# A decoder trunk in float32: the pools of SBUF tiles are placed in another order

## The chip, the cores and the metric

The kernel runs on 1 core of one Trainium2 chip. The metric is the device time of one execution in microseconds (us). Before the change it is 1981.16 us, the median of 3 runs (1981.11 to 1984.77).

## The reference, cut to what matters

Two layers work on `x` of 512 positions by 1024 channels. Everything is float32.

```python
for l in range(2):
    x = x + 0.5 * swiglu(rmsnorm(x, ln_ffn1[l]), w_ffn1_gu[l], w_ffn1_down[l])   # 1024 -> 2 x 2816 -> 1024
    h = rmsnorm(x, ln_mix[l])
    u_pool, q, k, v, gate_logits = split(h @ w_in[l])          # 512, 512, 128, 128, 2048 columns
    a = pool_mixer(u_pool, pool_w[l], pool_scale[l]) @ w_pool_branch[l]
    b = sliding_window_attention(rope(rmsnorm(q)), rope(rmsnorm(k)), v, sinks[l]) @ w_attn_branch[l]
    g_pool, g_attn = split(sigmoid(gate_logits))
    x = x + (g_pool * a + g_attn * b) @ w_out[l]
    x = x + 0.5 * swiglu(rmsnorm(x, ln_ffn2[l]), w_ffn2_gu[l], w_ffn2_down[l])
```

## The kernel before

`x` stays in SBUF as 8 tiles of 128 channels by 512 positions. Every large product is made of three matmuls: both operands are split into a high part (type float32r, a rounded float32) and a low part (what is left), and high times high, low times high and high times low are added up in PSUM (`term`, or the innermost loop of `product`). Names that end in `h` are high parts, in `l` low parts: `wh`, `wl` the weights, `xgh`, `xgl` the normed input, `hh`, `hl` the input of the down product, `ah`, `al` the attention's output, `yh`, `yl` the input of the output projection. `dh`, `dl` are the pool mixer's small products.

A matmul has a stationary operand, which is loaded into the array, and a moving operand, which streams past it column by column. In the rows of the trace a matmul reads `out<-moving,stationary`. Which one moves differs by stage:

- up product of an FFN (`product`, called by `block`): the weights move (512 or 384 columns), `xgh` and `xgl` are stationary. It uses seven products of half size in place of eight, and so some weight tiles are sums of others (`sums`). The qkv product is made the same way round with 256 columns.
- down product (`down`): `hh` and `hl` move (512 columns), the weights are stationary.
- `u` and gate products (`tile_of`): `xgh` and `xgl` move, the weights are stationary.
- branch products (the loop over `br` in `mix`): for each of 8 output tiles first four terms in which `ph` and `pl` move, then four in which `ah` and `al` move. `ph` and `pl` are the pool mixer's result; they lie behind the first 16 KB of the tiles `xgh` and `xgl` (`nm.spare`), and the trace shows them under those names.
- output product: `yh` and `yl` move.
- transposes (`turned`, `heads`, `attend`): the identity, a part of `cst`, moves, and what is transposed is stationary.

Weights come by DMA into a ring of six tiles `raw` (pool `rw`, SP's queue; the sums of two weight blocks by an adding DMA of POOL's queue). ScalarE casts them into `wh` (4 tiles in turn), VectorE subtracts into `wl` (3 tiles in turn). `Weights.prep` does this after each product for tiles some places ahead. At the end of each stage `Norm.split` makes the next stage's `xgh` and `xgl` out of each finished tile of `x`; `Norm.square` adds up the squares. Each stage has its pools: `ffn` opens `hp` (`hh`, `hl`), `ep`, `er` and `sums`, `mix` opens `mp` and `rp`, and they close with the stage. Engines work in the order in which the code is written, since every instruction is recorded with `keep_in_program_order` (line 90, which is the line in all rows).

A pool lies behind the pools that were opened before it. The built program places the tiles as in the table under "The change".

Of the kernel before, what the change touches and what calls it, by code (L numbers as in the profile page):

```python
# [9 lines left out]
F32 = mybir.dt.float32  # L10
F32R = mybir.dt.float32r
# [7 lines left out]
P = 128  # L19
L = 2  # L20
S = 512
# [3 lines left out]
HT = S // 2  # L25
# [5 lines left out]
NB = S // P  # L31
HQ = 8
HKV = 2
G = 4
HD = 64
# [5 lines left out]
TB = 6  # L41
RING = 16
RAW = 6
HI, LO = 4, 3
# [57 lines left out]
def trunk(ctx, tc, xT, consts, vecs, rows, w_g4, w_g3, w_d8, w_d6, w_qkv, w_u, w_pool, w_gate, w_br, w_out, out):  # L102
    nc = Engines(tc)
    pool = lambda name, bufs, **kw: ctx.enter_context(tc.tile_pool(name=name, bufs=bufs, **kw))
    cp, rw, wh_, wl_, xp = pool("cp", 1), pool("rw", RAW), pool("wh", HI), pool("wl", LO), pool("xp", 1)
    tp, sp = pool("tp", TB), pool("sp", 2)
    pa = pool("pa", 1, space=PSUM)

    cst = cp.tile([P, C_N], F32, name="cst")
# [21 lines left out]
    def temp(name, dt=F32):  # L131
        return tp.tile([P, S], dt, name=name, tag="t")

    def split(hi, lo, src, scale=None):

        if scale is None:
            nc.scalar.copy(out=hi, in_=src)
            nc.vector.tensor_tensor(out=lo, in0=src, in1=hi.bitcast(F32), op=ALU.subtract)
        else:
            nc.scalar.activation(out=hi, in_=src, func=AF.Copy, scale=scale)  # L140
            nc.vector.scalar_tensor_tensor(
                out=lo, in0=src, scalar=scale, in1=hi.bitcast(F32), op0=ALU.mult, op1=ALU.subtract
            )
# [165 lines left out]
    class Norm:  # L309
# [5 lines left out]
        def split(self, k):  # L315
            g = self.gain[:, k:k + 1]
            if self.h is None:
                self.h = xp.tile([P, 7 * 4 * HT], F32R, name="xgh")
                self.l = xp.tile([P, 7 * 4 * HT], F32R, name="xgl")
                self.spare = [t[:, KT * S:] for t in (self.h, self.l)]  # L320
                if self.halves:
                    self.h, self.l = (t.rearrange("p (i k t) -> p i k t", i=7, k=4) for t in (self.h, self.l))
                else:
                    self.h, self.l = (t[:, :KT * S].rearrange("p (k t) -> p k t", k=KT) for t in (self.h, self.l))
            if not self.halves:
                split(self.h[:, k, :], self.l[:, k, :], x[:, k, :], scale=g)
                return
            j = k % 4
            of = lambda i, n=1: (t[:, i:i + n, j, :] for t in (self.h, self.l))
            two = lambda t: t.rearrange("p (i t) -> p i t", t=HT)  # L330
            if k < 4:
                split(*of(B11), two(x[:, k, :])[:, 0:1, :], scale=g)
                d = temp("d")[:, :HT]
                nc.vector.tensor_tensor(out=d, in0=x[:, k, :HT], in1=x[:, k, HT:], op=ALU.subtract)
                split(*of(T1), two(d), scale=g)
                return
            xg, t, u = temp("xg"), temp("t23"), temp("t4")[:, :HT]
            gj = self.gain[:, j:j + 1]
            nc.scalar.activation(out=xg, in_=x[:, k, :], func=AF.Copy, scale=g)
            bh, bl = of(B21, 2)  # L340
            nc.scalar.copy(out=bh, in_=two(xg))
            nc.vector.scalar_tensor_tensor(
                out=t[:, HT:], in0=x[:, j, HT:], scalar=gj, in1=xg[:, HT:], op0=ALU.mult, op1=ALU.subtract
            )
            nc.vector.scalar_tensor_tensor(
                out=t[:, :HT], in0=x[:, j, :HT], scalar=gj, in1=t[:, HT:], op0=ALU.mult, op1=ALU.subtract
            )
            nc.vector.tensor_tensor(out=u, in0=xg[:, :HT], in1=t[:, :HT], op=ALU.subtract)
            nc.vector.tensor_tensor(out=bl, in0=two(xg), in1=bh.bitcast(F32), op=ALU.subtract)
            split(*of(T2, 2), two(t))  # L350
            split(*of(T4), two(u))
# [44 lines left out]
    def ffn(ctx, nm, nxt, last):  # L396
# [93 lines left out]
        def turned(src, b, base, n, hid, q):  # L490

            pt = pa.tile([P, S], F32, name=("pt_tp", "pt_pv")[q])
            for j in range(n // P):
                nc.tensor.transpose(pt[:, j * P:(j + 1) * P], src[:, j * P:(j + 1) * P], ident)
            split(
                *(t[:, base:base + n // P, b * P:(b + 1) * P] for t in hid),
                pt[:, :n].rearrange("p (j t) -> p j t", t=P),
            )
# [51 lines left out]

    @with_exitstack
    def mix(ctx, l, nm, nxt):
        mp = ctx.enter_context(tc.tile_pool(name="mp", bufs=1))
        rp = ctx.enter_context(tc.tile_pool(name="rp", bufs=RING))
        bank["mm"] = ctx.enter_context(tc.tile_pool(name="ps", bufs=4, space=PSUM))
        psc = ctx.enter_context(tc.tile_pool(name="psc", bufs=1, space=PSUM))
        gains = row[:, l, 0:HD], row[:, l, HD:2 * HD]
# [2 lines left out]

        wph, wpl = (t[:, 4 * S:5 * S] for t in nm.spare)
        us = [rp.tile([P, S], F32, name="u", tag="r") for _ in WIN]
        kv = mp.tile([P, NB, 4, HD], F32, name="kv")
        qT = mp.tile([P, G, S], F32, name="qT")
        kT = mp.tile([P, S], F32, name="kT")
        ph, pl = (t[:, :4 * S].rearrange("p (k t) -> p k t", k=4) for t in nm.spare)
        ah, al = (mp.tile([P, 4, S], F32R, name=n) for n in ("ah", "al"))
        nsink = sp.tile([P, HQ], F32, name="nsink")
        nc.vector.tensor_scalar(out=nsink, in0=sinks, scalar1=-1.0, scalar2=None, op0=ALU.mult)

# [3 lines left out]
        def window(g):  # L574

            w, cur, step = WIN[g], us[g], 1
            while step < w:
                nx = temp("win")
                nc.vector.tensor_copy(out=nx[:, :step], in_=cur[:, :step])
                nc.vector.tensor_tensor(out=nx[:, step:], in0=cur[:, step:], in1=cur[:, :S - step], op=ALU.add)  # L580
                cur, step = nx, step * 2
            yield
            nc.vector.tensor_tensor(
                out=cur[:, 0:16], in0=cur[:, 0:16], in1=cst[:, C_WC + g * 16:C_WC + (g + 1) * 16], op=ALU.mult
            )
            d = temp("d")
            nc.vector.scalar_tensor_tensor(
                out=d, in0=cur, scalar=1.0 / w, in1=us[g], op0=ALU.mult, op1=ALU.subtract
            )
            dh, dl = temp("dh", F32R), temp("dl", F32R)  # L590
            split(dh, dl, d)
            yield
            pt = mm()
            gemm(pt, [(wph[:, g * P:(g + 1) * P], wpl[:, g * P:(g + 1) * P], dh, dl)])
            yield
            split(ph[:, g, :], pl[:, g, :], pt, scale=vec[:, l, 3 * KT + g:3 * KT + g + 1])
            yield

        def rotate(z, n, cos, sin):
# [4 lines left out]
            nc.vector.tensor_tensor(out=rb[..., 0:8], in0=z[..., 8:16], in1=sin[..., 0:8], op=ALU.mult)  # L604
            nc.vector.tensor_tensor(out=rb[..., 8:16], in0=z[..., 0:8], in1=sin[..., 8:16], op=ALU.mult)
            nc.vector.tensor_tensor(out=z[..., 0:ROT], in0=ra, in1=rb, op=ALU.add)

        rs = mp.tile([P, NB, HQ], F32, name="hrs")

        ssq = mp.tile([P, NB, HQ], F32, name="hss")  # L610

        def sums(z, out):

# [242 lines left out]
    for l in range(L):  # L856
        nxt = Norm(gain(l, 1), False)
        ffn(nm, nxt, False)
        nm, nxt = nxt, Norm(gain(l, 2), True)
        mix(l, nm, nxt)  # L860
        nm, nxt = nxt, (Norm(gain(l + 1, 0), True) if l + 1 < L else None)
        ffn(nm, nxt, l + 1 == L)
        nm = nxt
# [72 lines left out]
```

## Time and profile before

| | |
|---|---|
| median of 3 runs | 1981.16 us |
| the profiled execution | 1982.2 us |
| its span (first to last instruction) | 1980.2 us |
| TensorE matmuls busy | 1920.4 us, 97% of the span |
| VectorE busy | 1304.4 us, 66% |
| ScalarE busy | 852.2 us, 43% |
| GpSimd busy | 132.9 us, 7% |
| mean granted clock of TensorE | 0.988 of full speed |
| HBM traffic | 130 GB/s |

How to read it: the profiled execution took 1.0 us more than the median, and 2.0 us of it lie outside the span. The duration of a single matmul in the rows contains its way through the array and overlaps with the next one's; what a matmul costs in a row of matmuls is the distance from its start to the next one's start. The chain that ended last gives that best: a piece of it is so many matmuls that follow one another without a wait, with the time that they took together.

### The profile page before, as it was taken

What the parts mean: (1) busy time and instruction counts of PE and PEld (TensorE: products, weight loads), DVE (VectorE), ACT (ScalarE), POOL (GpSimd) and SP (SyncE); (2) the same over time, 40 slices, a digit from 0 to 9 for tenths busy, and PEclk for the clock granted to TensorE, in tenths of its full rate; (3) what the DMA queues carried; (4) which work ended last, traced back from release to release, by engine and by line L of the source; (5) the groups of instructions that cost most, each with busy time, mean ns of one, the idle gap of its engine ahead of it and who ended that gap; (6) DMA issues with size and microseconds to landing.
All of it is one profiled execution on the core that took longest, in us unless ns stands there. A gap on an engine that the chain in (4) does not pass through costs nothing.

```text
span 1980.2 us, 24215 instructions
## 1 busy us (share of the span) xinstructions
PE 1920.4 (97%) x9240; PEld 1611.0 (81%) x9240; DVE 1304.4 (66%) x1884; ACT 852.2 (43%) x1286; POOL 132.9 (7%) x134
## 2 busy tenths in 40 slices
PE   3999999999999999999989999999999999999999
PEld 2788889897778788889868888898977877888897
DVE  5765747667756774756787476576765677657474
ACT  5433525445534542433454244244454454335242
POOL 3000000000001100000020000000000021000000
PEclk6999999999999999999999999999999999999999
DMA  5655546422224554646546564553222237455452
GB/s 173 178 148 150 160 107 160 128 92 75 75 86 117 149 160 128 181 120 148 134 119 179 140 172 124 127 154 119 90 64 86 85 87 204 139 151 165 117 157 78
DMA packets 77348, 258.48 MB, mean 131 GB/s; under 512 B 8720, under 2 KB 8720, under 8 KB 77232
## 3 DMA queue, kind: packets, MB, share of 16 engines
q1 hardware_dynamic: 63072, 210.27, 32.6%
q0 software_dynamic: 13872, 46.28, 13.9%
q8 instruction: 72, 1.18, 0.3%
q14 instruction: 44, 0.36, 0.1%
q10 hardware_dynamic: 288, 0.39, 0.1%
HBM read 254.81 MB, written 2.10 MB: 130 GB/s over the span
## 4 chain that ended last, share of the span: by engine, by line
PE 92%; DVE 5%; ACT 2%; issue 0%; DMA 0%; POOL 0%; SPq 0%; ACTq 0%; POOLq 0%
PE mm L90 86%; PE sc L90 3%; PE pt_pv L90 2%; PE pt_tp L90 2%; DVE wl L90 2%; DVE xgl L90 1%; ACT xgh L90 1%; DVE x L90 1%; DVE t L90 1%; DMA raw<-in_w_g 0%; DVE ssq L90 0%; ACT wh L90 0%; POOL ssq L90 0%; DVE v L90 0%; ACT xg L90 0%
## 5 line engine op out<-in xcount | busy, mean ns | idle before, releaser
L90 ACT CAST wh<-raw 128x1024 fp32r<-128x1024 f32 (+1 forms) x420 | 417.9, 995 | 567.6 <-PE mm L90 536.3
L90 DVE TENSOR_TENSOR wl<-raw,wh 128x1024 fp32r<-128x1024 f32 (+1 forms) x420 | 495.2, 1179 | 158.7 <-PE mm L90 83.3
L90 PE MATMUL mm<-wh,xgh 128*128 128x512 f32 (+2 forms) x1440 | 532.4, 370 | 25.4 <-DVE x L90 9.0
L90 PE MATMUL mm<-wl,xgh 128*128 128x512 f32 (+2 forms) x1440 | 529.1, 367 | 1.2 <-DVE wl L90 1.2
L90 PE MATMUL mm<-wh,xgl 128*128 128x512 f32 (+2 forms) x1440 | 528.7, 367 | 0.0
L90 PEld LDWEIGHTS mm<-wh,xgh 128*128 128x128 f32 x1440 | 272.7, 189 | 64.4 <-ACT wh L90 21.7
L90 PEld LDWEIGHTS mm<-wl,xgh 128*128 128x128 f32 x1440 | 272.8, 189 | 37.3 <-DVE wl L90 2.0
L90 PEld LDWEIGHTS mm<-wh,xgl 128*128 128x128 f32 x1440 | 272.6, 189 | 35.8
L90 PE MATMUL mm<-hh,wl 128*128 128x512 f32 x704 | 279.9, 398 | 2.6 <-DVE wl L90 2.6
L90 PE MATMUL mm<-hh,wh 128*128 128x512 f32 x704 | 281.6, 400 | 0.0
L90 PE MATMUL mm<-hl,wh 128*128 128x512 f32 x704 | 279.5, 397 | 0.0
L90 DVE SCALAR_TENSOR_TENSOR x<-mm,x 128x512 f32<-128x512 f32 x96 | 66.3, 690 | 215.3 <-PE mm L90 215.3
L90 POOL DMA_DIRECT2D raw<-in_w_g x96 | 82.1, 858 | 1700.9 <-DMA raw<-in_w_g 757.2
L90 ACT CAST wh<-sums 128x1024 fp32r<-128x1024 f32 (+1 forms) x96 | 94.1, 980 | 197.6 <-PE mm L90 140.7
L90 PEld LDWEIGHTS mm<-hh,wl 128*128 128x128 f32 x704 | 133.0, 189 | 35.8 <-DVE wl L90 3.5
L90 PEld LDWEIGHTS mm<-hh,wh 128*128 128x128 f32 x704 | 133.0, 189 | 31.2
L90 PEld LDWEIGHTS mm<-hl,wh 128*128 128x128 f32 x704 | 132.9, 189 | 31.3
L90 PE MATMUL mm<-xgh,wh 128*128 128x512 f32 x384 | 154.8, 403 | 1.8 <-DVE x L90 1.8
L90 PE MATMUL mm<-xgh,wl 128*128 128x512 f32 x384 | 150.1, 391 | 0.0
L90 PE MATMUL mm<-xgl,wh 128*128 128x512 f32 x384 | 149.9, 390 | 0.0
L90 DVE TENSOR_TENSOR wl<-sums,wh 128x1024 fp32r<-128x1024 f32 (+1 forms) x96 | 106.7, 1131 | 12.8 <-PE mm L90 12.6
L90 PEld LDWEIGHTS mm<-xgh,wh 128*128 128x128 f32 x384 | 72.1, 188 | 22.5 <-issue 8.2
(174 smaller groups left out, 1979.6 us busy)
## 6 DMA issues: line engine op xcount, KB each, us to landing
raw<-in_w_g SPq DMA_DIRECT2D x160, 512.0 KB, 3.9
raw<-in_w_g POOLq DMA_DIRECT2D x64, 512.0 KB, 6.2
raw<-in_w_d SPq DMA_DIRECT2D x64, 512.0 KB, 3.4
raw<-in_w_g SPq DMA_DIRECT2D x80, 384.0 KB, 3.2
raw<-in_w_gate SPq DMA_DIRECT2D x32, 512.0 KB, 3.5
raw<-in_w_g POOLq DMA_DIRECT2D x32, 384.0 KB, 5.1
raw<-in_w_d SPq DMA_DIRECT2D x32, 384.0 KB, 3.1
raw<-in_w_br SPq DMA_DIRECT2D x16, 512.0 KB, 3.5
```

Of the source, the lines that this page charges most:

```text
L90: return lambda *args, **kw: self.tc.keep_in_program_order(call(*args, **kw))
```

## The change

No instruction is added, removed or moved, and no wait: both built programs hold the same instructions in the same order on each engine, with the same semaphores and values. What differs is where tiles lie in a partition. The pools `wh`, `wl` and a new pool `xl` for `xgh` and `xgl` are opened first and on the left side, the other pools of the trunk on the right side, which fills the partition from its end. In `mix` the tiles `ah` and `al` get a pool of their own ahead of `rp` (`u`, `z`, `q`, `yh`, `yl`), and `rp` goes ahead of `mp`.

```diff
-    cp, rw, wh_, wl_, xp = pool("cp", 1), pool("rw", RAW), pool("wh", HI), pool("wl", LO), pool("xp", 1)
-    tp, sp = pool("tp", TB), pool("sp", 2)
+
+    wh_, wl_, xl = pool("wh", HI, side="left"), pool("wl", LO, side="left"), pool("xl", 1, side="left")
+    cp, rw, xp = pool("cp", 1, side="right"), pool("rw", RAW, side="right"), pool("xp", 1, side="right")
+    tp, sp = pool("tp", TB, side="right"), pool("sp", 2, side="right")
...
-                self.h = xp.tile([P, 7 * 4 * HT], F32R, name="xgh")
-                self.l = xp.tile([P, 7 * 4 * HT], F32R, name="xgl")
+                self.h = xl.tile([P, 7 * 4 * HT], F32R, name="xgh")
+                self.l = xl.tile([P, 7 * 4 * HT], F32R, name="xgl")
...
+        ap = ctx.enter_context(tc.tile_pool(name="ap", bufs=1))
+        ah, al = (ap.tile([P, 4, S], F32R, name=n) for n in ("ah", "al"))
+        rp = ctx.enter_context(tc.tile_pool(name="rp", bufs=RING))
         mp = ctx.enter_context(tc.tile_pool(name="mp", bufs=1))
-        rp = ctx.enter_context(tc.tile_pool(name="rp", bufs=RING))
```

The rest of the diff opens `rs`, `ssq` and `kv` in another order inside `mp`. Where the tiles lie, in KB (1024 bytes) from the start of a partition, by the built programs:

| tiles | moving operand in | before | after |
|---|---|---|---|
| `wh` (4), `wl` (3) | FFN up, qkv | 37.66 to 65.66 | 8.12 to 36.12 |
| `xgh` / `xgl` | `u`, gate, branch (`ph`, `pl`) | 81.66 to 109.66 / to 137.66 | 36.12 to 64.12 / to 92.12 |
| `hh` / `hl` | down | 160.81 / 176.81, each 16 long | 92.12 / 108.12 |
| `ah` / `al` | branch | 174.81 / 182.81, each 8 long | 92.12 / 100.12 |
| `yh`, `yl` (8 each, 2 long) | output | 191.06 to 223.06 | 108.12 to 140.12 |
| `dh`, `dl`, `p`, `diag` and other temporaries | small products | 141.69 to 153.69 | 162.41 to 174.41 |
| `cst` (identity, masks) | transposes | 8.12 to 10.88 | 218.44 to 221.19 |
| `v`, `r` (FFN), stationary in transposes | - | 200.81 to 212.81 | 132.12 to 144.12 |
| `x` | - | 65.66 to 81.66 | 174.41 to 190.41 |
| `raw` (6) | - | 13.66 to 37.66 | 194.44 to 218.44 |
| `sums` (2) | - | 212.81 to 220.81 | 144.12 to 152.12 |

The trunk's tiles before start 32 bytes past a multiple of 64 bytes up to and including `xgl`, and on a multiple of 64 from the temporaries on. After the change those of the first five rows start on a multiple of 64.

## Rows read from the trace of the kernel before

**Rows 1.** The page: busy time, share and instructions of each engine, and the chain that ended last by engine.

```profile
PE 1920.4 (97%) x9240; PEld 1611.0 (81%) x9240; DVE 1304.4 (66%) x1884; ACT 852.2 (43%) x1286; POOL 132.9 (7%) x134
PE 92%; DVE 5%; ACT 2%; issue 0%; DMA 0%; POOL 0%; SPq 0%; ACTq 0%; POOLq 0%
```

**Rows 2.** Groups of matmuls by form over the whole span: out<-moving,stationary, size, count, busy us, mean ns of one. Each product of a stage stands in three groups (high by high, low by high, high by low) of one count; one or two of them are shown.

```profile
L90 PE MATMUL mm<-wh,xgh 128*128 128x512 f32 x896 | 354.8, 396 | 25.4 <-DVE x L90 9.0 <-DVE v L90 5.9 <-ACT wh L90 5.8
L90 PE MATMUL mm<-hh,wh 128*128 128x512 f32 x704 | 281.6, 400 | 0.0
L90 PE MATMUL mm<-hl,wh 128*128 128x512 f32 x704 | 279.5, 397 | 0.0
L90 PE MATMUL mm<-xgh,wh 128*128 128x512 f32 x384 | 154.8, 403 | 1.8 <-DVE x L90 1.8
L90 PE MATMUL mm<-wh,xgh 128*128 128x384 f32 x448 | 150.4, 336 | 0.0
L90 PE MATMUL mm<-yh,wh 128*128 128x512 f32 x128 | 50.8, 396 | 0.0
L90 PE MATMUL mm<-wh,xgh 128*128 128x256 f32 x96 | 27.2, 283 | 0.0
L90 PE MATMUL mm<-ah,wh 128*128 128x512 f32 x64 | 25.2, 394 | 0.0
```

**Rows 3.** Pieces of the chain that ended last: start us, us, what, count of matmuls. The pieces are of an up product with 512 columns, of transposes, of an up product with 384 columns, of a qkv product with 256 columns, of the gate's last tile with the branch and the output products, and of the last down product.

```profile
90.55 32.67 PE mm L90 x144
123.22 0.44 PE pt_tp L90 x4
...
329.30 24.99 PE mm L90 x144
...
414.28 2.88 PE mm L90 x24
...
558.88 92.29 PE mm L90 x396
...
1946.97 29.53 PE mm L90 x126
```

**Rows 4.** TensorE in order of time in one tile of the branch product: start us, us. Nine matmuls with `ph` or `pl` moving (shown as `xgh`, `xgl`) lie between the first row and the first `ah` row, twelve with `ah` or `al` between that and the last row. The two `xgl` rows have their moving operand at 129.66 and 131.66 KB.

```profile
573.47 0.39 PE L90 MATMUL mm<-xgh,wh 128*128 128x512 f32 x1
...
574.37 0.39 PE L90 MATMUL mm<-xgl,wh 128*128 128x512 f32 x1
...
575.05 0.39 PE L90 MATMUL mm<-xgl,wh 128*128 128x512 f32 x1
...
575.50 0.40 PE L90 MATMUL mm<-ah,wh 128*128 128x512 f32 x1
...
578.31 0.39 PE L90 MATMUL mm<-xgh,wh 128*128 128x512 f32 x1
```

**Rows 5.** The same view in the gate product: three matmuls of the gate, three of the pool mixer (`dh`, `dl`, between 141.69 and 153.69 KB), and the next of the gate.

```profile
439.23 0.39 PE L90 MATMUL mm<-xgh,wh 128*128 128x512 f32 x1
...
439.90 0.40 PE L90 MATMUL mm<-dh,xgh 128*128 128x512 f32 x1
...
440.61 0.39 PE L90 MATMUL mm<-xgh,wh 128*128 128x512 f32 x1
```

**Rows 6.** Groups of VectorE's subtraction and of ScalarE's cast by form. `raw` lies at 13.66 to 37.66 KB, `sums` at 212.81 to 220.81 KB.

```profile
L90 DVE TENSOR_TENSOR wl<-raw,wh 128x1024 fp32r<-128x1024 f32 x308 | 385.3, 1251 | 119.3 <-PE mm L90 56.8 <-issue 27.9 <-ACT sa L90 15.6
L90 DVE TENSOR_TENSOR wl<-sums,wh 128x1024 fp32r<-128x1024 f32 x64 | 76.8, 1220 | 10.8 <-PE mm L90 10.6
...
L90 ACT CAST wh<-raw 128x1024 fp32r<-128x1024 f32 x308 | 324.1, 1052 | 445.8 <-PE mm L90 416.2 <-PE sc L90 11.9 <-issue 7.0
L90 ACT CAST wh<-sums 128x1024 fp32r<-128x1024 f32 x64 | 67.3, 1052 | 129.1 <-PE mm L90 82.3 <-DVE sums L90 46.8
```

**Rows 7.** DMA issues: what, queue, count, size of one, median us from issue to landing. `praw` lies among the temporaries.

```profile
raw<-in_w_g SPq DMA_DIRECT2D x160, 512.0 KB, 3.9
...
praw<-in_w_pool SPq DMA_DIRECT2D x2, 256.0 KB, 3.8
```

**Rows 8.** The chain that ended last at the end of the first FFN (to 390.20) and at the end of layer 0's second FFN: start us, us, what.

```profile
364.05 0.70 DVE x L90
...
389.40 0.66 DVE x L90
390.06 0.14 issue
390.20 1.86 PE mm L90 x7
...
976.18 0.70 DVE x L90
...
1012.49 0.61 DVE x L90
1013.24 3.71 PE mm L90 x8
```

**Rows 9.** Stretches: from:to us, length, busy time of PE, PEld, DVE, ACT and POOL, PEclk (granted clock as a share of full speed), DMA share, GB/s.

```profile
965.00:1023.00 58.00, 48.05 (x201) 38.25 (x200) 44.09 (x68) 29.21 (x50) 13.36 (x9) 0.91 0.34 95
...
1630.00:1645.00 15.00, 12.75 (x53) 10.37 (x52) 10.96 (x20) 8.40 (x10) 1.96 (x3) 0.89 0.69 162
```

More of the change, by code (lines that the diff above doesn't have):

```diff
@@ L562, in mix @@
         us = [rp.tile([P, S], F32, name="u", tag="r") for _ in WIN]
-        kv = mp.tile([P, NB, 4, HD], F32, name="kv")
+        rs = mp.tile([P, NB, HQ], F32, name="hrs")
+        ssq = mp.tile([P, NB, HQ], F32, name="hss")
         qT = mp.tile([P, G, S], F32, name="qT")
@@ L566, in mix @@
         ph, pl = (t[:, :4 * S].rearrange("p (k t) -> p k t", k=4) for t in nm.spare)
-        ah, al = (mp.tile([P, 4, S], F32R, name=n) for n in ("ah", "al"))
+        kv = mp.tile([P, NB, 4, HD], F32, name="kv")
         nsink = sp.tile([P, HQ], F32, name="nsink")
@@ L606, in rotate @@
             nc.vector.tensor_tensor(out=z[..., 0:ROT], in0=ra, in1=rb, op=ALU.add)
-        rs = mp.tile([P, NB, HQ], F32, name="hrs")
-        ssq = mp.tile([P, NB, HQ], F32, name="hss")
         def sums(z, out):
```

## The prediction, made before the changed kernel was run

> **What bounds the kernel now.** I read the page first: its busy times and its chain by engine. TensorE's matmuls fill 97% of the span and make 92% of the chain that ended last; VectorE is at 66%, ScalarE at 43% [rows 1]. So the price of a matmul in a row of matmuls is what the kernel pays, and the forms tell how many there are of each [rows 2]. Their mean durations (396, 400, 403 ns) overlap and say little. The pieces of the chain give the spacing [rows 3]. An up product with 512 columns (the weights move, from 37 to 66 KB) takes 32.67 us for 144 matmuls, 226.9 ns each. The last down product (`hh` and `hl` move, from 160 to 193 KB) takes 29.53 us for 126 with as many columns, 234.4 ns each. Neither piece holds a wait, so the 7.5 ns are TensorE's own.
>
> Is it the place, or the kind of product? The branch product answers: weights stationary, 512 columns, one PSUM tile after another, and only the moving operand changes in the middle. Nine matmuls with `ph` and `pl` take 575.50 - 573.47 = 2.03 us, 226 ns each; the twelve with `ah` and `al` (175 to 191 KB) that follow take 578.31 - 575.50 = 2.81 us, 234 ns each [rows 4]. The pool mixer's `dh` and `dl` (142 to 154 KB) show the same: three take 0.71 us, 237 ns each, after three of the gate's in 0.67 us [rows 5]. Moving operands that begin at 141 KB or more are slow, those from 37 to 134 KB are fast. The two `pl` rows at 129.66 and 131.66 KB lie above 128 KB, each between two low ones, and the nine show no delay [rows 4]: the edge is not sharply at 128 KB, or one such matmul alone is hidden.
>
> **The change part by part.**
>
> *Matmuls whose moving operand comes down.* Down: 3 x 704 = 2112. Output: 3 x 128 = 384. Branch, attention's half: 3 x 64 = 192 [rows 2]. 2688 in all, at 234.4 - 226.9 = 7.5 ns: -20.2 us. A check on the largest mixed piece: 12 gate and 96 `ph`/`pl` matmuls at 226.9 ns and 96 + 192 others at 234.4 ns make 92.0 us, the piece has 92.29 [rows 3].
>
> *The tail of `yh` and `yl`.* Six of the sixteen tiles lie above 128 KB afterwards, two of them above 136 KB. Each of the eight pairs has 48 of the 384 matmuls. If the edge is at 128 KB, three pairs stay slow: 144 x 7.5 = 1.1 us. By the `pl` rows only the pair at 136 and 138 KB is in doubt: 48 x 7.5 = 0.4 us. I take +0.4, with 0 and 1.1 as its ends.
>
> *Matmuls whose moving operand goes up.* `cst` goes from 8 to 218 KB; the transposes use it, 128 columns each, some 450 of them, 0.44 / 4 = 110 ns each [rows 3]. If the extra time goes with the columns, 7.5 x 128 / 512 = 1.9 ns, that is +0.9 us at most. Against it, what they load as the stationary operand (`v`, `r`) comes down by 60 KB; no row shows what that is worth, and 1.9 ns each is its bound too. I take 0, between -0.9 and +0.9. Matmuls with `kT`, `p`, `dh`, `dl` or `diag` stay above 140 KB: 0.
>
> *The stationary operands.* `wh`, `wl`, `xgh`, `xgl` go down; `xgl` as a stationary operand already lies on both sides of 128 KB in the up products that run at 226.9 ns: 0.
>
> *VectorE and ScalarE.* `raw`, `x` and `cst` go up. The subtraction takes 1251 ns from `raw` (low) and 1220 from `sums` (high), the cast 1052 from either [rows 6]: the place matters by 31 ns of 1251 at most, on engines that have a third of the span and more to spare [rows 1]. Where VectorE is on the path (below), some seven tiles each, that is 3 x 7 x 31 ns = 0.7 us either way. I take 0.
>
> *DMA.* `raw` is written at 194 to 218 KB. Landing takes 3.9 us for 512 KB into the low `raw` and 3.8 us for 256 KB into `praw` at 142 to 154 KB [rows 7]. Even twice that is covered: six tiles are in the ring, a down tile lasts 24 x 227 ns = 5.4 us, and DMA is 0% of the chain [rows 1]. 0.
>
> *What VectorE gives back.* At two kinds of place TensorE's gain cannot reach the end, because the chain runs through `x`, `Norm.split` and `wl` on VectorE and ScalarE without a matmul: at the end of each first FFN, from 364.05 to 389.40, and at the end of layer 0's second FFN, from 976.18 to 1012.49 [rows 8]. The down product issues some 108 matmuls in each (six tiles of 18), so 108 x 7.5 = 0.8 us of the gain end in a longer wait of TensorE: three times 0.8 = +2.4 us. The lower end is 0 (the chain also begins earlier with a faster down product, and the first FFN's stretch is nearly a tie: PE's last matmuls end there too), the upper end 2.4. I take 2.4, since the chain has no PE in it.
>
> Sum: -20.2 + 0.4 + 2.4 = -17.4 us, in the profiled execution 1982.2 -> 1964.8 us. That execution lies 1.0 us above the median; the median goes from 1981.2 to **1963.8 us**, 0.9% faster.
>
> *A rule against it.* The rows put 7.5 ns on the place of the moving operand [rows 3, 4]. The Trainium skill, "TensorE: Matmul & The Clock Gate", section "Back-to-back issue gap", has the spacing of warm matmuls as the columns over the clock plus a fixed 2.5 ns, with no place in memory in it: 216 ns for 512 columns. By that rule the change is worth 0 and the time stays 1981.2. The trace doesn't agree: neither 226.9 nor 234.4 is 216, and two levels stand side by side in one product.
>
> **The rivals.**
>
> *1. The bottom of the partition is not fast, or it is not the height at all.* The lowest fast row is `wh` at 37.66 KB. Afterwards `wh` and `wl` lie at 8 to 36 KB, where so far only `cst` is streamed, in transposes for which there is no other place to compare. If that part is slow, the moving weights lose: 2688 matmuls of 512 columns at 7.5 ns = 20.2, 1344 of 384 at 5.6 = 7.6, 576 of 256 at 3.8 = 2.2, together +30.0 us [rows 2, 3]. With the gain of 17.4 that is 1981.2 + 12.6 = **1993.8**. It turns the sign once `wh` is caught (two in three of these matmuls, 20 us): an edge above 24 KB does it. A second form: all moving operands at 227 ns begin 32 bytes past a multiple of 64, all at 234 ns on it, and afterwards all begin on it. Then nothing is gained, and the weights and the 1152 matmuls with `xgh` or `xgl` moving (8.6 us) get slow: 1981.2 + 38.6 = **2019.8**. For it: the trace cannot tell the two apart. Against the second form: a misaligned stream that is faster than an aligned one would be odd. On the first, `cst` at 8 KB streams in transposes at 110 ns [rows 3], and no row of that form elsewhere says whether this is fast.
>
> *2. The place is not the cause, and nothing changes*: 1981. It needs something else that goes with `hh`, `ah`, `yh` and `dh` alike and not with `ph` in the same product. I see only that all of them were written shortly before; but so were `wh` and `wl`.
>
> *3. Only part comes through.* The edge lies lower for some tiles (`hl` ends at 124 KB, `yh` at 140), or faster down products run into the weights' preparation. For the second: the ends of stages already run on VectorE [rows 8]; against it, over the whole span it has a third to spare [rows 1]. Half the gain: **1972**.
>
> *The clock* is no rival but a spread: stalls at the end of layer 0 and at the second FFN of layer 1 bring stretches with a granted clock of 0.91 and 0.89, matmuls at the lower of its two levels, 1.2 GHz [rows 9]. Over 15 us, 0.89 is 3.3 us at half speed, 1.7 us lost. One such stretch more or less is +-1.7 us.
>
> **How the numbers follow.** Forecast 0.74; rival 1, both forms, 0.09; rival 2, 0.08; rival 3, 0.09. The forecast's own ends: all of 20.2 + 0.9 us through and one slow stretch of the clock less gives 1981.2 - 22.8 = 1958.4; the tail at 1.1, transposes at +0.9, and one more slow stretch gives 1963.8 + 0.7 + 0.9 + 1.7 = 1967.1. Down to rival 3's 1972 the range is **1958 to 1972**, which leaves out rivals 1 and 2. About 0.2% (4 us) is what a measurement of this kernel can tell from no change: its three runs lie 3.7 us apart. Faster 0.83 (forecast and rival 3), same 0.08, slower 0.09.
>
> **What the profile of the changed kernel would show.** Right: the last down product's 126 matmuls in 28.6 us in place of 29.53; the up product's 144 still in 32.7; the piece of 396 in 90.1, or 90.7 with three pairs of `y` slow; DVE's and ACT's means within 1%; longer waits of PE at the ends of the first FFNs. Rival 1: the up product's piece of 144 goes to 33.7 us (and in its second form the gate's to 234 ns, with the down product unchanged). Rival 2: no piece changes. Rival 3: the pieces are shorter, but waits of PE on DVE `wl` or on ACT `wh` grow by several us, or the down pieces lie between 28.6 and 29.5. Wrong altogether would be a change in DMA landing or in VectorE's means that reaches the chain.

## The result, and the profile after

The changed kernel takes 1965.62 us (median of 4 runs, 1962.26 to 1966.46), the kernel before 1981.13 us beside it (4 runs): a ratio of 0.9915, 95% interval 0.9898 to 0.9932. That is 15.5 us less, 1.8 us more than the 1963.8 us predicted, and inside the range. The profiled execution is the shortest of the four (1962.26 us, span 1960.2 us, 20.0 us less than the span before). The time came out as forecast; the reason that the prediction gave for it, the height of the data in the partition, did not hold, as the experiments show.

The page of the kernel after has TensorE 20.9 us less busy; VectorE is the same to 2.0 us, ScalarE to 1.8 us, and the chain has more VectorE in it than [rows 1].

```profile
PE 1899.5 (97%) x9240; PEld 1608.9 (82%) x9240; DVE 1302.4 (66%) x1884; ACT 850.4 (43%) x1286; POOL 132.8 (7%) x134
PE 89%; DVE 8%; ACT 2%; issue 0%; DMA 0%; POOL 0%; SPq 0%; ACTq 0%; POOLq 0%
```

The chain's pieces that answer to [rows 3], start us, us, what, count: the up product of 144 and the last down product.

```profile
88.39 32.70 PE mm L90 x144
...
403.41 2.88 PE mm L90 x24
...
1927.95 28.60 PE mm L90 x126
```

The down product's 126 matmuls take 28.60 us, 227.0 ns each, where they took 234.4; the up product and the q, k and v products have not moved. The matmuls on `ah`, `al`, `yh` and `yl` stand 226 to 227 ns apart too, the last tiles of `y` above 128 KB among them. One product did not get faster, and its rows, TensorE in order of time, answer to [rows 5]: three matmuls of the pool mixer still take 0.70 us, 233 ns each.

```profile
434.80 0.40 PE L90 MATMUL mm<-dh,xgh 128*128 128x512 f32 x1
...
435.50 0.39 PE L90 MATMUL mm<-xgh,wh 128*128 128x512 f32 x1
```

At the end of the first FFN the chain runs through VectorE as in [rows 8], and TensorE's wait (the bracket: idle before, and releaser) is 1.64 us, where the same row of before says 0.88. The first row below is of after, the second of before. (Where the expectations below give 1.80 and 1.05 us, they count from the start of the matmul before, less the usual 227 ns.)

```profile
385.12 0.47 PE L90 MATMUL mm<-xgh,wh 128*128 128x512 f32 x1 [1.64 <-DVE x L90]
```

```profile
390.20 0.47 PE L90 MATMUL mm<-xgh,wh 128*128 128x512 f32 x1 [0.88 <-DVE x L90]
```

### The profile page after: what moved, and what is told of

Its sections match the earlier page's. It is cut to its first block, busy times and chain, and to the rows that moved or that the text cites. A ratio compares the mean times of both kernels' runs of the same rounds, so it can differ in the third digit from the quotient of the medians.

```text
span 1960.2 us, 24215 instructions
## 1 busy us (share of the span) xinstructions
PE 1899.5 (97%) x9240; PEld 1608.9 (82%) x9240; DVE 1302.4 (66%) x1884; ACT 850.4 (43%) x1286; POOL 132.8 (7%) x134
## 4 chain that ended last, share of the span: by engine, by line
PE 89%; DVE 8%; ACT 2%; issue 0%; DMA 0%; POOL 0%; SPq 0%; ACTq 0%; POOLq 0%
PE mm L90 83%; PE sc L90 3%; DVE wl L90 2%; DVE xgl L90 2%; PE pt_pv L90 2%; PE pt_tp L90 2%; DVE x L90 1%; ACT xgh L90 1%; DVE t L90 1%; ACT xg L90 0%; DVE ssq L90 0%; ACT wh L90 0%; DMA raw<-in_w_g 0%; POOL ssq L90 0%; DVE v L90 0%
## 5 line engine op out<-in xcount | busy, mean ns | idle before, releaser
L90 PE MATMUL mm<-hh,wl 128*128 128x512 f32 x704 | 274.5, 390 | 2.6 <-DVE wl L90 2.6
L90 PE MATMUL mm<-hh,wh 128*128 128x512 f32 x704 | 276.2, 392 | 0.0
L90 PE MATMUL mm<-hl,wh 128*128 128x512 f32 x704 | 273.9, 389 | 0.0
```

The lines of the kernel that those rows point to most:

```text
L90: return lambda *args, **kw: self.tc.keep_in_program_order(call(*args, **kw))
```

## The experiments

**The height by itself.** The first run leaves the computation out: it streams 24 or 48 matmuls at a time, of float32r with 512 columns unless said otherwise, from operands at known places (`w`, the stationary one, at 12 KB).

```
for kb, t in at.items():
    for h in range(2):
        run("m%03dkb" % (kb + 2 * h), [(t[:, h * 512:h * 512 + 512], w)])
...
run("p32lo", [(lo[:, 8:520], w)])
run("p32hi", [(hi[:, 8:520], w)])
```

> A kernel that leaves the whole computation out: it fills 4 KB tiles over the partition from 8 to 216 KB with x, runs matmuls on them and copies x to the output. Nearly all have 512 columns of float32r, a fresh stationary load each, 24 to a group; a group m130kb has its moving operand from 130.1 to 132.1 KB, and the stationary operand stays at 12 KB. Place theory: groups up to m138kb are spaced at 227 ns, from some edge between 140 and 142 KB on at 234 ns. Rival, an edge at 128 KB: 234 ns from m128kb on. Rival, the phase within 64 bytes: all groups begin on a multiple of 64 plus 0, so all at 234 ns, and p32lo and p32hi, which begin 32 bytes later, both at 227 ns; the place theory has p32lo at 227 and p32hi at 234. If the extra time goes by the column, groups c128, c256, c384 differ between lo (44 KB) and hi (196 KB) by 1.9, 3.8 and 5.6 ns; if it is paid once for each matmul, by 7.5 ns each. onehi moves one operand in three from 196 KB, twohi two in three: without hiding the mean of three is 229 and 232 ns, with hiding 227. s012kb to s204kb move 128 columns and vary the stationary operand's place: no difference if only the moving operand counts. bflo and bfhi are bfloat16, f32lo and f32hi plain float32.

The chain of this run, one piece for each group. The two p32 rows are the ones whose moving operand begins 32 bytes further on, at 44 KB and at 196 KB; in the last row the moving operand is at 196 KB and the stationary one at 204 KB.

```profile
20.35 5.44 PE m008kb L23 x24
...
335.87 5.44 PE m128kb L23 x24
...
379.39 5.44 PE m144kb L23 x24
...
558.91 5.44 PE m214kb L23 x24
...
686.98 5.60 PE p32lo L23 x24
692.58 5.60 PE p32hi L23 x24
...
768.44 5.44 PE shihi L23 x24
```

5.44 / 24 = 226.7 ns at every height from 8 to 214 KB: the theory of the height falls. The place of the stationary operand does not count either: 110.6 to 111.7 ns for 128 columns at seven places, and the same 226.7 ns for 512 columns with it at 204 KB. What costs is 32 bytes: 5.60 / 24 = 233.3 ns, low and high alike. Neither bfloat16 (215.8 ns) nor float32 (24 matmuls in 20.60 us, 858 ns each, which the trace shows as 48 rows 429 ns apart) depends on the height; whether 32 bytes cost them anything was not tried here.

**The edge at 128 KB.** `hh` and `hl` at 120 to 152 KB, by opening their pool after the others.

```diff
-        hp = ctx.enter_context(tc.tile_pool(name="hp", bufs=1))
...
+        hp = ctx.enter_context(tc.tile_pool(name="hp", bufs=1))
```

> The changed kernel with the FFN's pools opened in another order, so that hh lies at 120 to 136 KB and hl at 136 to 152. Place theory with an edge between 140 and 142 KB: only hl's slices from 140 or 142 KB on get 7.5 ns longer, 416 to 512 matmuls, 3.1 to 3.8 us: 1968.7 to 1969.5 us. Edge at 128 KB: also hh's upper half and all of hl, 1344 matmuls, 10.1 us: 1975.7 us. If a single such matmul between two low ones is hidden: 1965.6 us, no change, with the last down product's 126 matmuls in 28.6 us.

1965.28 us, ratio 0.9917 (0.9902 to 0.9932), the same as after, with the last down product's 126 again in 28.60 us. There is no edge here. (A single high matmul hidden between two low ones would give the same; the sweep's 24 high ones in a row, at 226.7 ns, exclude that.)

**The weights high.** `wh` and `wl` at 190 to 218 KB, `raw` low.

```diff
-    wh_, wl_, xl = pool("wh", HI, side="left"), pool("wl", LO, side="left"), pool("xl", 1, side="left")
-    cp, rw, xp = pool("cp", 1, side="right"), pool("rw", RAW, side="right"), pool("xp", 1, side="right")
+    rw, xl = pool("rw", RAW, side="left"), pool("xl", 1, side="left")
+    cp, wh_, wl_ = pool("cp", 1, side="right"), pool("wh", HI, side="right"), pool("wl", LO, side="right")
+    xp = pool("xp", 1, side="right")
```

> The changed kernel with wh and wl at 190 to 218 KB and raw at 8 to 32 KB; hh, hl, ah, al, yh, yl stay low. Place theory: the weights are the moving operand in the up and qkv products, 2688 matmuls of 512 columns at 7.5 ns, 1344 of 384 at 5.6 and 576 of 256 at 3.8 make 30.0 us: 1995.6 us, the up product's piece of 144 in 33.7 us, down, gate and output unchanged though their stationary operand lies high. Rival, that it depends on which data moves (results of the vector engines but lately written) and not on the place: 1965.6 us.

1989.49 us, ratio 1.0037 (1.0024 to 1.0051). Slower, but in the wrong products: the rows are an up product (weights moving), a q, k and v product (weights moving, 256 columns) and the last down product, where the weights are stationary and the moving `hh` and `hl` lie low as in after.

```profile
90.02 32.98 PE mm L90 x144
...
405.81 2.72 PE sc L90 x24
...
1953.58 29.42 PE mm L90 x126
```

The down product lost all that the change had given it (233.5 ns) with its moving operand low; the up product lost only 2 ns of the 7.5 expected; and the 256-column products got faster, 113.3 ns where they take 120.0 in [rows 3] and after. No rule on heights gives these three. In the addresses as built, the weights begin here at 192 modulo 256 (the remainder when the address in bytes is divided by 256), and what they meet in these products begins at 128.

**Start instead of height.** Two runs separate them. In the kernel before, 96 unused bytes ahead of the temporaries: everything stays high, but `hh`, `ah` and `yh` begin where the weights begin, modulo 128 (and modulo 256: both at 160). In the kernel after, 32 unused bytes ahead of the stage pools (the line stands once in each of the two stages): everything stays low, but the starts differ by 32.

```diff
+    pool("pad", 1).tile([P, 24], F32, name="pad")
```

> The kernel before with one unused tile of 96 bytes ahead of the temporaries: every tile of the stages moves up by 96 bytes and stays above 141 KB (hh at 160.9 KB, ah at 174.9, yh at 191.2); their start then leaves 32 when divided by 128, as that of the weights does. Theory after the first four runs: what counts is the start of the moving operand against that of the stationary operand, 32 bytes apart in the kernel before (64 against 32) and equal in the changed one. Then this kernel gets the whole gain with all data high: 1965.6 us, the last down product's 126 matmuls in 28.6 us. Height theory of the prediction: no change, 1981.2 us and 29.5 us.

```diff
+        ctx.enter_context(tc.tile_pool(name="pad", bufs=1)).tile([P, 8], F32, name="pad")
```

> The changed kernel with an unused tile of 32 bytes ahead of the stage's pools: all moving operands stay below 141 KB, but those of the down, output and attention's branch products start 32 bytes past a multiple of 128, the weights on it. Relative start theory: the gain is gone, 1965.6 + 16 to 20 = 1981 to 1986 us, the last down product's 126 matmuls in 29.5 us. Height theory: no change, 1965.6 us, 28.6 us.

Before with 96 bytes: 1966.69 us, ratio 0.9923 (0.9908 to 0.9937). The whole gain, with nothing moved down. After with 32 bytes: 1978.23 us, ratio 0.9987 (0.9978 to 0.9997). Most of it gone, with everything low; 3.3 us under before are left where the expectation had none, and 2688 matmuls at 233.5 in place of 234.4 ns make 2.4 of them. The last down product says the same; the first row is of before with 96 bytes, the second of after with 32.

```profile
1933.06 28.60 PE mm L90 x126
```

```profile
1941.15 29.42 PE mm L90 x126
```

**Which starts.** The computation is left out again: 36 matmuls for each shift, first of the moving operand against the stationary one (m), then of the stationary operand (s), then of both (b), then with fewer columns and other types.

```
for d in (0, 4, 8, 16, 32, 48, 64, 80, 96, 112, 128, 160, 192, 224, 256, 320, 384, 448, 512, 1024):
    run("m%04db" % d, mv, st, 512, d, 0, 36)
...
for d in (16, 32, 48, 64, 96, 128, 192, 256, 512):
    run("s%04db" % d, mv, st, 512, 0, d, 36)
...
for d in (16, 32, 64, 96):
    run("b%04db" % d, mv, st, 512, d, d, 36)
```

> A kernel that leaves the whole computation out: four tiles low in the partition, filled from x, and groups of 36 matmuls with a fresh stationary load each. m0032b moves its operand from 32 bytes further on, the stationary operand stays; s0032b the other way round; b0032b both. 512 columns of float32r; n384x, n256x and n128x have fewer columns, bf bfloat16, fp plain float32. Relative start theory: b groups and m0000b at 227 ns, m0032b and s0032b near 233, and the pattern over the shifts repeats with some period (128 or 256 bytes); n256x0064b at 113 ns in place of 120, as the qkv product took with the weights 64 bytes past xgh. If only the moving operand's own start counted, s groups are all 227 and b groups vary. Height theory: all 227.

The chain, a piece for each group, with the shift in bytes in the name:

```profile
19.14 8.16 PE m0000b L23 x36
27.30 8.52 PE m0004b L23 x36
...
52.55 8.40 PE m0032b L23 x36
...
69.34 8.24 PE m0064b L23 x36
...
111.00 8.43 PE m0160b L23 x36
119.43 8.40 PE m0192b L23 x36
...
144.41 8.26 PE m0320b L23 x36
...
177.65 8.16 PE m1024b L23 x36
...
191.25 8.17 PE s0016b L23 x36
199.41 8.39 PE s0032b L23 x36
...
241.39 8.24 PE s0192b L23 x36
...
271.39 8.28 PE b0016b L23 x36
279.67 8.21 PE b0032b L23 x36
```

8.16 / 36 = 226.7 ns where the starts agree, 233.3 at 32 bytes and at 192, 234.2 at 160, 236.6 at 4, and only 228.8 at 64. 320 costs about what 64 costs (8.26 and 8.24) and 1024 nothing, so the pattern repeats every 256 bytes. Shifting the stationary operand alone costs the same, by the difference: 192 back is 64 ahead (8.24 in both). Shifting both by 32, 64 or 96 gives 227.5 to 228.1 over a group and 226.7 in its second half. Two shifts by 16 show that the difference is not quite all: the stationary operand alone 16 bytes on costs nothing (8.17), both 16 on cost 230.0 ns (8.28); no operand of these kernels begins there. Shifts change bfloat16 (215.8 ns) and float32 (858 ns a matmul, again in two rows) not at all, and 128 columns neither (111.6). For the starts that the kernels have, multiples of 32, the spacing of float32r matmuls goes with (moving start minus stationary start) modulo 256.

With this the earlier runs fall into place:

| kernel, product | difference of starts mod 256 | ns each, 512 columns |
|---|---|---|
| before: down, output, branch | 64 - 160 = -96, that is 160 | 234.4 |
| before: pool mixer; after: the same | 192 - 160 = 32; 160 - 128 = 32 | 237; 233 |
| after, before with 96 bytes: down | 0 | 227.0 |
| after with 32 bytes: down | 32 | 233.5 |
| weights high: down; up | 128 - 192 = -64, that is 192; 192 - 128 = 64 | 233.5; 229.0 |

The sweep has 234.2 at 160, 233.3 at 32 and 192, and 228.8 at 64. Why the difference counts, and why modulo 256, no run shows.

**A start that helps.** If the difference rules, 64 bytes ahead should make the q, k and v products of the changed kernel faster, as it did with the weights high. Their weights are placed 64 bytes further on in tiles made 256 bytes longer; a smaller `ones` and a warm-up tile put among the temporaries make room.

```diff
-                self.hi.append(wh_.tile([P, CH], F32R, name="wh"))
+                self.hi.append(self.place(wh_.tile([P, CH + 64], F32R, name="wh"), c))
...
+        def place(self, t, c):
+            at = 16 if c["kind"] == "qkv" else 0
+            return t[:, at:at + CH]
...
```

> The kernel after, with the weights of the q, k and v products alone (256 columns, moving operand) placed 64 bytes further on inside their tiles, so that the moving start is 64 ahead of the stationary start modulo 256 bytes there and equal to it everywhere else. Theory of the relative start: the 256-column matmuls, 120.0 ns when both starts are equal, take 113.3 ns (as in the run with the weights high, whose weights also began 64 ahead) or 117.8 ns (as in the sweep of starts at 64): 576 of them give 3.9 or 1.3 us, so 1961.7 to 1964.3 us, and the chain's pieces of 24 q, k and v matmuls become 2.72 to 2.83 us long instead of 2.88. Rival, that only an operand's own start or its height counts, or that 256-column matmuls are bound elsewhere: pieces of 2.88 and 1965.6 us.

1961.57 us (1959.10 to 1962.49), ratio to before 0.9902 (0.9887 to 0.9917): 4.0 us under after's median, whose interval overlaps with this one; the rows decide. The twenty-four matmuls take 2.72 us where they took 2.88, and 24 such pieces make 3.8 us.

```profile
405.18 2.72 PE mm L90 x24
```

In the sweep the same shift gave 117.8 ns, not 113.3; there 113.3 came at a shift of 112 bytes. Which property of the kernel's stream makes the difference was not settled.

**What the ends of stages wait for.** The prediction let VectorE keep part of the gain where the chain has no matmul. To shorten VectorE's chain there, its additions of squares went to GpSimd.

```diff
-                e = nc.gpsimd if self.halves else nc.vector
+                e = nc.gpsimd
```

> The changed kernel with the adding up of squares at the end of the first FFNs on GpSimd in place of VectorE. Theory that VectorE's chain there keeps TensorE's gain back (TensorE's wait at these two ends grew from 1.05 us to 1.80 and 1.79 us): with 0.69 us less on VectorE for each of 8 tiles the waits fall to 1.05 us or less, 1.5 us or more in all: 1964.1 us or less. Rival, that the wait is for ScalarE's cast or the last matmul: waits and time unchanged, 1965.6 us.

1975.96 us, ratio 0.9974 (0.9964 to 0.9983): 10.3 us slower than after, which neither the expectation nor its rival had. First a subtraction in the chain at the end of the first FFN in after, then the same in this kernel, the addition beside it on GpSimd (in order of time), and TensorE's wait:

```profile
375.74 0.87 DVE wl L90
```

```profile
374.73 1.98 DVE wl L90
```

```profile
374.61 1.29 POOL L90 TENSOR_TENSOR ssq<-ssq,sq 128x512 f32<-128x512 f32 x1 [2.84 <-ACT sq L90]
```

```profile
390.36 0.77 PE L90 MATMUL mm<-xgh,wh 128*128 128x512 f32 x1 [4.70 <-DVE x L90]
```

The 0.60 us of an addition left VectorE, and the subtraction took 1.11 us more; six tiles of 0.51 us net are the 3.1 us by which the wait grew from 1.64 us. The second of the two first FFNs ends alike (4.69 us), which makes 6.1 of the 10.3 us. Most of the rest lies right behind these waits, in the next 24 matmuls; after first, then this kernel:

```profile
385.12 5.73 PE mm L90 x24
```

```profile
390.36 8.22 PE mm L90 x24
```

Behind the longer wait the granted clock is 0.50, the lower level of 1.2 GHz, from 390 to 394 us, where after has 1.00 from 385 to 389. That costs 2.5 us here and 2.0 behind the other wait (7.76 against 5.73). The run shows that VectorE sets this end, and that GpSimd is no free helper. The Trainium skill, "SBUF — State Buffer", section "Who interferes with whom", has a VectorE instruction with two inputs in SBUF contend with a GpSimd instruction that reads SBUF; the 1.98 us beside 0.87 agree.

**Squares on VectorE alone.** If GpSimd's additions slow VectorE, taking them all away should help at the start and at the end of layer 0, where they stand.

```diff
-                e = nc.gpsimd if self.halves else nc.vector
+                e = nc.vector
```

> The kernel after, with every addition of squares on VectorE, and none on GpSimd. Theory that GpSimd's additions slow VectorE's subtractions of two operands: at the end of layer 0's second feed-forward the low parts beside GpSimd's additions lose their 2.0 to 2.7 us in the chain, and a pair of tiles takes some 9.5 instead of 11.15 us: 5.8 us less; at the start four GpSimd additions that stand in the chain (7.07 us) become some 2.8 us on VectorE: 4.3 us less; together about 1955.6 us. Rival: VectorE gets the work that GpSimd had and is the engine waited for there, so the ends get no shorter: 1965 us or more.

1959.94 us (1958.11 to 1961.19), ratio 0.9895 (0.9880 to 0.9910): 5.7 us under after's median, not 10. The intervals overlap, before was 1.05 us faster beside this run than beside after, and the profiled executions (this kernel's longest, after's shortest) lie only 1.1 us apart, so the rows decide. At the start, GpSimd's four additions stood in the chain of after from 35.93 to 42.95, and TensorE's first long row of matmuls began at 44.87; now it begins at 41.00. The chain of after, then of this kernel:

```profile
35.93 2.12 POOL ssq L90
...
44.87 23.69 PE mm L90 x96
```

```profile
36.71 0.70 DVE ssq L90
...
41.00 24.96 PE mm L90 x96
```

At the end of layer 0 the expectation failed. The subtractions there lost their extra (0.87 to 1.14 us, where after has 1.94 to 2.23 in three of eight), but the additions and their squares entered the chain. From the first `x` to the 96 matmuls behind the norm after takes 1012.52 - 968.62 = 43.90 us, this kernel 1010.49 - 964.93 = 45.56. The chain of after, then of this kernel:

```profile
968.62 0.70 DVE x L90
...
986.29 1.94 DVE wl L90
...
1012.52 22.08 PE mm L90 x96
```

```profile
964.93 0.70 DVE x L90
...
977.26 0.62 ACT sq L90
977.91 0.69 DVE ssq L90
978.60 0.87 DVE wl L90
...
1010.49 21.90 PE mm L90 x96
```

The rival was right for this place.

**Both, and the additions late.** The shifted q, k and v weights, and each addition on VectorE one tile late, while it waits for ScalarE.

```diff
+        def add(self):
+            if self.late is not None:
+                nc.vector.tensor_tensor(out=self.acc, in0=self.acc, in1=self.late, op=ALU.add)
+                self.late = None
...
-                e.tensor_tensor(out=self.acc, in0=self.acc, in1=sq, op=ALU.add)
+                self.late = sq
...
```

> Both of the above, and each addition of squares done one tile late on VectorE, while it waits for ScalarE's high part of the next tile. Theory: 3.9 us (or 1.3) from the q, k and v products, 10 us from the ends as above, and TensorE's waits at the ends of both first feed-forwards down from 1.80 to some 1.05 us each, 1.5 us: about 1950 us (1953 with the smaller price). Rival: the late addition delays the low part that the matmuls wait for, and the waits at the ends stay at 1.80 us or grow: 1955 us or more.

1955.31 us (1953.66 to 1956.13), ratio 0.9869 (0.9853 to 0.9886): faster than both kernels, by 25 us and 10 us, but 5 us short of the expectation. TensorE's wait at the end of the first FFN is back at the 0.88 us of before, so the late additions no longer hold it up:

```profile
380.27 0.47 PE L90 MATMUL mm<-xgh,wh 128*128 128x512 f32 x1 [0.88 <-DVE x L90]
```

What fell short is again the end of layer 0: from 962.29 to 1007.34, 45.05 us, 1.15 more than after where about 5.8 less were expected, and the 96 matmuls behind it take 23.66 us where after's take 22.08.

```profile
1007.34 23.66 PE mm L90 x96
```

## Why the prediction was right in time and wrong in cause

- **The term of -20.2 us, right in size.** 2688 matmuls from 234.4 to 227.0 ns are 19.9 us. The price was read from two rows of the same kernel, and any cause that took all of these matmuls from one row to the other would have given it. That is why the time came out with the cause wrong.
- **"Is it the place?", the step that failed.** The prediction saw that slow operands lay from 141 KB up and fast ones below 134 KB, and took the height for the cause. Height and start went together in that kernel: `hh`, `ah`, `yh` began 160 bytes (modulo 256) past their weights, `dh` 32, and only operands that began with their partner were fast. The two `pl` rows at 129 and 131 KB, put down to an unsharp edge, were fast for that reason [rows 4]. The change moved the pools, and the new addresses happened to agree modulo 256, which the prediction had not asked of them: that was luck. It would have gained as much where it was (before with 96 bytes: 1966.69), and little low with other starts (after with 32 bytes: 1978.23).
- **Rival 1.** Its first form, a slow bottom of the partition, falls with the 226.7 ns at 8 KB. Its second form asked the right question, whether the start counts, and gave it part of 0.09. It compared each start with a fixed grid, where the other operand of the same matmul is what counts; its 2019.8 us came from that. Rival 2 (something that goes with `hh`, `ah`, `yh` and `dh`, not with `ph`) described the cause without naming it; only its price, no change, was wrong.
- **The tail of `y`, +0.4:** it was 0; all tiles of `y` run at 227 ns.
- **VectorE gives back 2.4: right in size.** In the profiled runs, TensorE's wait at the ends of the two first FFNs grew from 0.88 to 1.64 and 1.63 us, 1.5 us in all against 1.6 for these two. At layer 0's end the stretch from the first `x` to the 96 matmuls takes 1021.99 - 976.18 = 45.81 us in before, and 1014.38 - 968.63 = 45.75 in the kernel with `hh` at the edge, whose matmuls are as fast as after's: VectorE kept all of the 0.8 us there. Rows of before, then of the kernel with `hh` at the edge:

```profile
984.62 2.71 DVE wl L90
...
1021.99 22.07 PE mm L90 x96
```

```profile
968.63 0.70 DVE x L90
...
977.05 2.70 DVE wl L90
...
1014.38 22.13 PE mm L90 x96
```

- **What the prediction did not have.** After's own stretch is 43.90 us, because the subtraction that takes 2.71 us in before takes 0.87 (at 977.03). This 1.8 us is not the faster matmuls' doing: besides the kernel at the edge (2.70), before with 96 bytes is as fast in them and has 2.62 us there, while after with 32 bytes is slow in them and has 0.87. What decides it stays open.
- **The terms put at nothing** stayed there: four transposes take 0.44 us in both kernels, VectorE's subtraction from `raw` 1255 ns where it took 1251, and DMA is 0% of the chain. (`v` and `r` came down by 69 KB, not 60.)
- **The sum.** -19.9 + 1.5 + 0.8 - 1.8 = -19.4 us, and a start that came 1.1 us earlier with the first weights, against -20.0 of the profiled spans. Stretches of the lower clock level nearly cancel: the 96 matmuls behind layer 0's mixing stage take 24.90 us in after and 22.07 in before (granted clock 0.91 and 1.00 from 640 to 680), while the same row at the start is 1.1 us shorter than in before and the one in layer 1 1.7. The medians differ by 15.5: the other three executions of after are 3.1 to 4.2 us longer than the profiled one. Their granted clock is 0.987, 0.987 and 0.986 against 0.988, and 0.001 of 1960 us is 2 us, so the clock can hold this; without their traces it is not shown.
- **The rule against the change.** The Trainium skill, "TensorE: Matmul & The Clock Gate", section "Back-to-back issue gap", gives 512 columns 216 ns, which it calls the gap of an isolated matmul, and about 131 ns in a stream; neither has a term for a place. bfloat16 agrees with the first (215.8 ns in a stream), and no run here shows the second. That the height costs nothing agrees too; but float32r stands at 226.7 at best, and the starts, which the rule does not have, made the change worth 15.5 us.

## What to carry to other kernels

When slow and fast instructions differ in where their data lies, list the addresses of both operands and their difference before calling it height: a pad of some bytes is the cheaper experiment, and here it was worth the whole change. Give float32r operands that meet in a matmul of 512 columns the same start modulo 256 bytes, and recheck it whenever a pool moves. A price read from the trace can be right while its cause is wrong, and an edit built on that cause then fails: the kernel after with 32 bytes kept everything low and lost most of the gain.

## What the runs showed of the hardware that was not expected

- float32r with 512 columns: 226.7 ns when both operands start alike modulo 256 bytes (230.0 with both 16 bytes on), 226.9 with the stationary one 16 bytes ahead, 228.8 with the moving one 64 ahead, 231 to 237 at the other differences tried. 256 columns: 120.0 ns at equal starts, and 113.3 with the moving operand 64 bytes ahead in the three kernels that had it so (117.8 in the sweep), so there equal starts are not the best; 384 columns move by less than 4 ns (173.3 to 176.7), 128 columns not at all.
- The height in the partition costs nothing: 226.7 ns from 8 to 214 KB for the moving operand, and the stationary one was tried from 12 to 204 KB.
- A VectorE subtraction of 128x768 takes 0.87 us in the chain alone and 1.98 beside a GpSimd addition of 1.29 us.
- TensorE's waits of 4.70 and 4.69 us were each followed by some 4 us at a granted clock of 0.50, which cost 2.5 and 2.0 us more; behind waits of 1.64 and 1.63 us the clock stayed at 1.00.
